# Up and down groups of an MLP woven job by job, with one more block pair of each up group in seven products

## The chip, the cores and the metric

The kernel runs on one NeuronCore of a Trainium2 chip. The metric is the device time of one execution in microseconds (us); for the kernel before it is the median of three runs. Engines are named as in the profile: PE (TensorE, matmuls), PEld (its weight loads), DVE (VectorE), ACT (ScalarE), POOL (GpSimd), SP (SyncE, which issues the DMAs).

## The reference

One layer of a trunk on x of 256 tokens by 2048 channels, float32. Two groups of heads (differential attention and an RWKV-7 recurrence) share one input projection, and one output projection adds to x; a squared-ReLU MLP follows.

```python
h = rms_norm(x, norm_mix[l])
proj = jnp.einsum('btd,de->bte', h, w_in[l])
...
mixed = jnp.concatenate([a_out, y], axis=-1)
x = x + jnp.einsum('bte,ed->btd', mixed, w_out[l])
h2 = rms_norm(x, norm_mlp[l])
u = jnp.square(jax.nn.relu(jnp.einsum('btd,df->btf', h2, mlp_up[l])))
x = x + jnp.einsum('btf,fd->btd', u, mlp_down[l])
```

D_MODEL is 2048 and D_FF 8192; mlp_up is 2048 x 8192 and mlp_down 8192 x 2048.

## The kernel before

**Split products.** Every weight is loaded as a float32 tile raw of 256 rows by 512 columns (a job; on chip 128 partitions x 1024). ACT casts it to hi, DVE subtracts to lo, and activations are kept as a high and a low unit in the same way. A product of a 128-row block is three matmuls: high by hi, high by lo, low by hi. A plain job is two row blocks by two halves of the tokens by three matmuls: 12 matmuls of 512 columns (`gemm`, L571). There are four tiles raw (NRAW) and three each of hi and lo (LOOK + 1).

**Seven products.** For the up projection's column groups from the fourth on (QUICK = 3), the jobs whose number within the group stands in FAST are done by a scheme of seven block products in place of eight (`seven`, L545): 21 matmuls of 256 columns. For them `split` (L517) builds, on DVE, four sums T of the weight's quarters, casts them to Th on ACT and subtracts to Tl on DVE; `normal_h` (L1449) builds the sums S of the activations once for each FAST job. The group then has four PSUM banks, and `join` (L1483) adds them up into C.

**Groups.** An up group i (16 of them, 8 jobs) makes 512 columns of the hidden layer: PE's products, a ReLU into z, a transpose, a square and the split into a unit u. A down group (32 of them, 4 jobs) multiplies two units u with a block of mlp_down and adds 256 x 512 results to x2. In the kernel before, the program writes whole groups one after the other: up, down, down, up, down, down.

**Order.** The program only records instructions (Recorder, L65). `plan` (L195) then sets the order of every engine's queue with costs and latencies of its own: it takes the instruction that can start first by its clock, and among those that could start at once the lowest rank. What `split` records has its rank lowered by SPL, so it goes ahead. Matmuls of attention and recurrence (transposes of tiles, small products, all in banks sm and tr) are side products that the plan puts between the main ones. An instruction with an anchor cannot be planned before the PE instruction that was recorded last before it; anchors bind instructions under hold and some DMAs.

Names in rows: raw, hi, lo, T, Th, Tl as above; xT, hT, hN, y, a, u are activation units; acc and side are PSUM banks of main products, four each, and sm and tr share the side banks; v, Am, Rm, X, UV, ao, pr belong to the recurrence and the attention; sq and sums to the first norm.

Of the kernel before, what the change touches and what calls it, by code (L numbers as in the profile page):

```python
# [14 lines left out]
F32R = mybir.dt.float32r  # L15
# [17 lines left out]
NRAW = 4  # L33
LOOK = 2
EV = 13
FAST = (1, 2, 4, 5, 7)
QUICK = 3

SPL = 120
KEEP = 0.3  # L40
WIN = 1.5
BD = 2.0
BA = 2.0

# [74 lines left out]
class Op:  # L119
    def __init__(self, eng, fname, fn, args, kw, rank):  # L120
        self.eng, self.fname, self.fn, self.args, self.kw, self.rank = eng, fname, fn, args, kw, rank
        aps = [a for a in args if isinstance(a, bass.AP)]
        self.outs = [aps[0]] + [kw[k] for k in ("accum_out",) if kw.get(k) is not None]
        self.ins = aps[1:] + [v for k, v in kw.items() if isinstance(v, bass.AP) and k != "accum_out"]
        n = int(np.prod(list(aps[0].shape)[1:]))
        self.dma = 0
        if fname == "dma_start":
            self.dma = n * aps[0].shape[0] * 4
            self.cost = 0.45
            self.small = min(a.ap[-1][1] for a in aps[:2]) < 128  # L130
        elif eng == "tensor":
            if fname == "transpose":
                self.cost = 0.11
            elif aps[1].dtype in (F32R, BF16):
                self.cost = 0.0056 + max(n, 64) * 0.000443
            else:
                m = aps[1].shape[-1]
                self.cost = 0.008 + max(n, m) * 0.00166
                if m <= 64:
                    self.cost = 0.06  # L140
        elif eng == "vector":
            m = int(np.prod(list(aps[1].shape)[1:])) if len(aps) > 1 else n
            single = fname in ("tensor_scalar", "tensor_copy") and aps[1].space != PSUM
            self.cost = 0.068 + max(n, m) * (0.00052 if single else 0.0063 if fname == "reciprocal" else 0.00104)
            if fname == "tensor_scalar" and aps[1].space == PSUM:
                self.cost += 0.16
            if fname == "tensor_tensor_scan":
                self.cost += 0.25
            if fname == "scalar_tensor_tensor" and len(aps) > 3:
                self.cost += 0.05  # L150
        elif eng == "scalar":
            self.table = {AF.Sqrt: 1, AF.Tanh: 2, AF.Exp: 2}.get(kw.get('func', args[2] if len(args) > 2 else None), 0) if fname == 'activation' else 0
            self.cost = (0.065 if aps[1].space == PSUM else 0.095) + n * 0.000833 + 0.085 * (len(self.ins) - 1 + len(self.outs) - 1)
            if aps[0].shape[0] <= 64:
                self.cost += 0.11
        else:
            self.cost = 0.1 + n * 0.001
        self.deps, self.users, self.left, self.ready = set(), [], 0, 0.0
        self.tiles = []
        self.bulk = eng == "tensor" and fname == "matmul" and aps[1].dtype == F32R and n == 512  # L160
        if eng == "tensor":
            self.load = min(1.0, n * (0.000417 if aps[1].dtype in (F32R, BF16) else 0.00083 if fname == "transpose" else 0.00167) / self.cost)
            self.load *= aps[1].shape[0] / P


class Together:
    def __init__(self, parts, rank):
        self.eng, self.fname, self.parts, self.rank, self.dma, self.bulk = "tensor", "together", parts, rank, 0, False
# [26 lines left out]
def plan(ops):  # L195
# [3 lines left out]
    tiles = {}  # L199
    for i, op in enumerate(ops):  # L200
        op.i = i
        if op.anchor and (op.hold or op.dma and op.outs[0].tensor.name.split("_")[0] != "raw"):
            op.deps.add(op.anchor)
        for write, aps in ((False, op.ins), (True, op.outs)):
            for ap in aps:
# [53 lines left out]
    while len(out) < len(ops):  # L259
# [77 lines left out]
def record(ctx, tc, A, nc):  # L337
# [138 lines left out]
                advance(t)  # L476

    w_in, w_out, w_up, w_dn = A["w_in"], A["w_out"], A["up"], A["down"]
    turn = [0]
# [11 lines left out]
    def fast(job):  # L491
        return job[0] is w_up and job[2] >= 512 * QUICK and job[1] // 256 in FAST

    jobs += up_jobs(0) + up_jobs(1)
    for e in range(8):
        for j in range(4):
            if e < 7 and not j % 2:
                jobs += up_jobs(2 * e + 2 + j // 2)
            jobs += [(w_dn, e * 1024 + 256 * k, 512 * j, 512) for k in range(4)]
    raws, parts = deque(), deque()  # L500

    def load(between=None):
# [42 lines left out]
    def seven(acc, u, k, S, B, first, last):  # L545
# [6 lines left out]
            return [u[:, i, k + kk, t * P:(t + 1) * P] for i in range(2)]  # L552

        def s(i):
            return [S[:, j, i] for j in range(2)]

        def b(kk, n):
            return [x[:, kk, n * 256:n * 256 + 256] for x in (hi, lo)]
# [12 lines left out]
    def gemm(units, w, c0, ncols, evac, side=False, hooks={}, off=0):  # L571
        turn[0] += w is w_up or w is w_dn
        quick = [j for j in range(8) if fast((w, 256 * j, c0))]
        acc = [bank("side" if turn[0] % 2 else "acc") for _ in range(4 if quick else 2)]
        nu = 4 if w is not w_out and w is not w_dn else 2
        nh = 2 * nu
        for j in range(nh):
# [8 lines left out]
            if j in quick:  # L586
                seven(acc, units[j // 2], 2 * j % 4, sums_[FAST.index(j)], (hi, lo, *T_), j == quick[0], j == quick[-1])
                done(2)
                continue
            for kk in range(2):  # L590
                k = 2 * j + kk
                u = units[off + j // 2]
                for t in range(2):
# [4 lines left out]
                    nc.tensor.matmul(o, xh, hi[:, kk, :ncols], start=(k == 0), stop=False, **more)  # L598
                    nc.tensor.matmul(o, xh, lo[:, kk, :ncols], start=False, stop=False, **more)
                    nc.tensor.matmul(o, xl, hi[:, kk, :ncols], start=False, stop=(k == 2 * nh - 1), **more)  # L600
        evac(acc)

    def rsqrt_small(out, ss, scale, bias):

# [827 lines left out]
        squares(x2[j], parts2, j)  # L1432

    rows2 = []

    def rstd_rows():

# [11 lines left out]
    def normal_h(j):  # L1449
# [7 lines left out]
        for p in range(2):  # L1457
            if 2 * j + p in FAST:

                S, sr = ftile([P, 2, 4, P], "S", F32R), ftile([P, 4, P], "sr")  # L1460
# [5 lines left out]
                nc.scalar.copy(S[:, 0], sr)  # L1466
                nc.vector.tensor_sub(S[:, 1], sr, S[:, 0])
                sums_.append(S)
                done()
        done()  # L1470
# [6 lines left out]
    us = []  # L1477
    pend = []

    def up_group(i, hooks):  # L1480
# [48 lines left out]
        gemm(hN if i > 1 else hT, w_up, 512 * i, 512, f, hooks=hooks)  # L1529

    def store_evac(j):
        def f(acc):
# [12 lines left out]
    for e in range(8):  # L1545
        for j in range(4):
            if e < 7 and not j % 2:
# [92 lines left out]
```

## Time and profile before

| | us |
|---|---|
| median of three runs | 1192.0 (1191.72 to 1192.01) |
| the profiled execution | 1192.01 |
| its span on the core | 1190.2 |
| PE busy in the span | 1179.4 |
| PEld busy | 979.9 |
| DVE busy | 974.1 |
| ACT busy | 844.8 |

The granted TensorE clock is full in all forty slices of the page. A share of busy time is a mean over stages. PE's ends are modelled: a matmul of 512 columns shows some 0.39 us and the next one starts 0.23 us later, so rates are read from the starts. The start comes first (weights and x arrive), then the projections with attention and recurrence in between, up to some 490 us, then the MLP.

### The profile page before, as it was taken

What the parts mean: (1) busy time and instruction counts of PE and PEld (TensorE: products, weight loads), DVE (VectorE), ACT (ScalarE), POOL (GpSimd) and SP (SyncE); (2) the same over time, 40 slices, a digit from 0 to 9 for tenths busy, and PEclk for the clock granted to TensorE, in tenths of its full rate; (3) what the DMA queues carried; (4) which work ended last, traced back from release to release, by engine and by line L of the source; (5) the groups of instructions that cost most, each with busy time, mean ns of one, the idle gap of its engine ahead of it and who ended that gap; (6) DMA issues with size and microseconds to landing.
All of it is one profiled execution on the core that took longest, in us unless ns stands there. A gap on an engine that the chain in (4) does not pass through costs nothing.

```text
span 1190.2 us, 18141 instructions
## 1 busy us (share of the span) xinstructions
PE 1179.4 (99%) x6649; PEld 979.9 (82%) x6649; DVE 974.1 (82%) x1579; ACT 844.8 (71%) x1421; POOL 7.3 (1%) x31
## 2 busy tenths in 40 slices
PE   9999999999999999999999999999999999999998
PEld 6887887888778778788888888888888888888886
DVE  7789594896975976798988988988988998898864
ACT  7784566855687768999686777687677677677652
POOL 2000000000000000000000000000000000000000
PEclk9999999999999999999999999999999999999999
DMA  8655656256455445656666666666666666666663
GB/s 279 205 159 164 172 162 184 85 165 175 128 169 172 141 142 184 180 169 194 188 198 199 184 203 198 194 190 197 212 176 196 198 192 182 208 180 197 207 205 132
DMA packets 126297, 216.20 MB, mean 182 GB/s; under 512 B 21824, under 2 KB 24384, under 8 KB 126208
## 3 DMA queue, kind: packets, MB, share of 16 engines
q1 hardware_dynamic: 126208, 215.05, 60.0%
q8 instruction: 52, 0.85, 0.3%
q14 instruction: 37, 0.30, 0.1%
HBM read 211.09 MB, written 3.93 MB: 181 GB/s over the span
## 4 chain that ended last, share of the span: by engine, by line
PE 77%; DVE 10%; ACT 7%; DMA 3%; issue 3%; SPq 0%; DVEq 0%; ACTq 0%
PE acc L334 47%; PE side L334 23%; DVE lo L334 4%; PE sm L334 3%; PE tr L334 3%; ACT z L334 2%; ACT hi L334 2%; DVE Tl L334 2%; DVE T L334 2%; PE sm L179 2%; DMA raw<-up 1%; DMA raw<-w_in 1%; DVE x L334 1%; DVE uf L334 0%; DVE u L334 0%
## 5 line engine op out<-in xcount | busy, mean ns | idle before, releaser
L334 DVE TENSOR_TENSOR lo<-raw,hi 128x1024 fp32r<-128x1024 f32 (+3 forms) x460 | 462.7, 1015 | 151.3 <-ACT hi L334 148.7
L334 ACT CAST hi<-raw 128x1024 fp32r<-128x1024 f32 (+2 forms) x395 | 405.0, 1033 | 164.2 <-PE acc L334 106.8
L334 PE MATMUL acc<-hi,xT 128*128 128x512 f32 (+1 forms) x832 | 267.6, 396 | 0.6 <-ACT hi L334 0.6
L334 PEld LDWEIGHTS acc<-hi,xT 128*128 128x128 f32 x832 | 154.6, 190 | 33.8 <-ACT hi L334 1.7
L334 PE MATMUL acc<-lo,xT 128*128 128x512 f32 (+1 forms) x416 | 164.0, 394 | 0.7 <-DVE lo L334 0.6
L334 PE MATMUL acc<-hi,u 128*128 128x512 f32 x512 | 163.2, 395 | 0.0
L334 PE MATMUL side<-hi,u 128*128 128x512 f32 x512 | 163.1, 395 | 0.0
L334 ACT ACTIVATE z<-C 32x128 f32<-32x128 f32 x338 | 104.2, 308 | 39.4 <-DVE C L334 35.0
L334 ACT CAST Th<-T 128x1024 fp32r<-128x1024 f32 x65 | 68.2, 1050 | 71.0 <-DVE T L334 70.3
L334 PEld LDWEIGHTS acc<-hi,u 128*128 128x128 f32 x512 | 96.4, 188 | 22.4 <-DVE u L334 0.3
L334 PEld LDWEIGHTS side<-hi,u 128*128 128x128 f32 x512 | 96.5, 188 | 22.2
L334 PE MATMUL side<-lo,u 128*128 128x512 f32 x256 | 101.0, 395 | 0.0
L334 PE MATMUL acc<-lo,u 128*128 128x512 f32 x256 | 101.0, 394 | 0.0
L334 PEld LDWEIGHTS acc<-lo,xT 128*128 128x128 f32 x416 | 78.9, 190 | 18.2 <-DVE lo L334 2.2
L334 PE MATMUL side<-hi,hN 128*128 128x512 f32 (+1 forms) x328 | 91.7, 353 | 0.0
L334 PE MATMUL acc<-hi,hN 128*128 128x512 f32 (+1 forms) x308 | 83.4, 343 | 0.0
L334 DVE TENSOR_TENSOR Tl<-T,Th 128x1024 fp32r<-128x1024 f32 x65 | 79.1, 1216 | 0.0
L334 PEld LDWEIGHTS side<-hi,hN 128*128 128x128 f32 x328 | 59.7, 188 | 9.5
L334 PEld LDWEIGHTS acc<-hi,hN 128*128 128x128 f32 x308 | 55.5, 188 | 7.8
L334 PE MATMUL side<-lo,hN 128*128 128x512 f32 (+1 forms) x164 | 57.9, 353 | 0.0
L334 PEld LDWEIGHTS acc<-lo,u 128*128 128x128 f32 x256 | 48.2, 188 | 11.0
L334 PEld LDWEIGHTS side<-lo,u 128*128 128x128 f32 x256 | 48.2, 188 | 11.0
(310 smaller groups left out, 1874.0 us busy)
## 6 DMA issues: line engine op xcount, KB each, us to landing
raw<-up SPq DMA_DIRECT2D x128, 512.0 KB, 3.8
raw<-down SPq DMA_DIRECT2D x128, 512.0 KB, 4.4
raw<-w_in SPq DMA_DIRECT2D x93, 512.0 KB, 3.8
raw<-w_out SPq DMA_DIRECT2D x32, 512.0 KB, 3.9
raw<-w_in SPq DMA_DIRECT2D x8, 288.0 KB, 3.1
x<-x SPq DMA_DIRECT2D x4, 512.0 KB, 7.3
out<-x SPq DMA_DIRECT2D x8, 256.0 KB, 3.4
raw<-w_in SPq DMA_DIRECT2D x6, 256.0 KB, 5.8
```

Source lines behind the costliest of these rows:

```text
L179: p.fn(*p.args, **p.kw)
L334: op.fn(*op.args, **op.kw)
```

## The change

- FAST has six of eight jobs (1, 2, 3, 5, 6, 7) in place of five (1, 2, 4, 5, 7). Two of the six sums S live in small tiles that the recurrence has left (HOME).
- `gemm` becomes a generator `steps` that stops after each job. From the fourth up group on, one up group and two down groups (three beside the last two) are run job by job in an order written as a string of u and d; the loads follow the same order. The first three up groups run alone, the last four down groups too. Up groups use the banks acc (the second one side), down groups the banks side; before, groups took the two kinds in turn.
- `join` is ranked like `split`, and its last two additions of 256 columns become one of 512 whose PSUM operand is repeated.
- In `plan`, POOL's instructions (memsets that clear tiles) get anchors. A side product whose operand comes from another engine than PE is planned to be ready LATE = 1.0 us later than its operand.

```diff
-FAST = (1, 2, 4, 5, 7)
+FAST = (1, 2, 3, 5, 6, 7)
...
+LATE = 1.0
...
+        self.side = eng == "tensor" and not (fname == "matmul" and aps[2].tensor.name.split("_")[0] in ("hi", "lo", "Th", "Tl"))
...
-        if op.anchor and (op.hold or op.dma and op.outs[0].tensor.name.split("_")[0] != "raw"):
+        if op.anchor and (op.hold or op.eng == "gpsimd" or op.dma and op.outs[0].tensor.name.split("_")[0] != "raw"):
             op.deps.add(op.anchor)
...
-            u.ready = max(u.ready, done + lag(op, u.eng))
+            u.ready = max(u.ready, done + lag(op, u.eng) + (LATE if u.side and op.eng != "tensor" else 0.0))
...
+    def beside(i):
+        a = 2 * i - 6 + (i > 14)
+        return list(range(a, a + 2 + (i > 13))), ("ddududuududududu" if i < 14 else "dddududduddududuudud" if i < 15 else "dduduuduuduududddddd")
+    for i in range(3):
+        jobs += up_jobs(i)
+    for i in range(3, 16):
+        ds, order = beside(i)
+        ups, downs = up_jobs(i), [j for d in ds for j in down_jobs(d)]
+        jobs += [(ups if c == "u" else downs).pop(0) for c in order]
+    for d in range(28, 32):
+        jobs += down_jobs(d)
...
-        acc = [bank("side" if turn[0] % 2 else "acc") for _ in range(4 if quick else 2)]
+        acc = [bank(tag) for _ in range(4 if quick else 2)]
...
+            if j < nh - 1:
+                yield
         evac(acc)
+        yield
...
+                if len(sums_) in HOME:
+                    S = [sm.tile([P, 512], F32R, tag=g, bufs=1, name=nm("S")).rearrange("p (s t) -> p s t", s=4) for g in HOME[len(sums_)]]
...
+            nc.rank = -SPL
             nc.scalar.copy(q[:, 0], b2[:, lt])
...
-            nc.vector.tensor_add(C[:, 1, lt], C[:, 1, lt], b3[:, rt])
-            nc.vector.tensor_add(C[:, 1, rt], C[:, 1, rt], b3[:, rt])
+            c1 = C[:, 1].rearrange("p (n c) -> p n c", n=2)
+            nc.vector.tensor_add(c1, c1, b3[:, rt].unsqueeze(1).broadcast_to([P, 2, 256]))
+            nc.rank = 0
...
-    up_group(0, {2: lambda: make_h(3), 4: rstd_rows})
-    up_group(1, {2 * j: lambda j=j: normal_h(j) for j in range(4)})
...
-    for e in range(8):
-        for j in range(4):
-            if e < 7 and not j % 2:
-                up_group(2 * e + 2 + j // 2, {1: fin_hook})
-            gemm(us, w_dn, 512 * j, 512, store_evac(j) if e == 7 else add_evac(x2[j]), hooks={1: fin_hook}, off=2 * e)
+    for _ in up_group(2, {1: fin_hook}):
+        pass
+    for i in range(3, 16):
+        ds, order = beside(i)
+        gens = {"u": up_group(i, {}), "d": run(*(down_group(d) for d in ds))}
+        for c in order:
+            next(gens[c])
+    for _ in run(*(down_group(d) for d in range(28, 32))):
+        pass
```

How the order moves, at three places. First PE in the middle of an MLP group, at the end of a job in seven products (its last block product is Th and Tl by hN). Before, the next job in seven products of the same up group follows:

```order
L334 MATMUL side_1685<-Th_1700,hN_1070 128x256
L334 MATMUL side_1685<-Tl_1701,hN_1070 128x256
L334 MATMUL side_1685<-Th_1700,hN_1070 128x256
L334 MATMUL side_1686<-hi_1703,hN_1070 128x256
L334 MATMUL side_1686<-lo_1704,hN_1070 128x256
```

Now, after two such jobs, a job of a down group stands there:

```order
L337 MATMUL acc_1687<-Th_1708,hN_1062 128x256
L337 MATMUL acc_1687<-Tl_1709,hN_1062 128x256
L337 MATMUL acc_1687<-Th_1708,hN_1062 128x256
L337 MATMUL side_1717<-hi_1711,u_1447 128x512
L337 MATMUL side_1717<-lo_1712,u_1447 128x512
```

Up and down jobs of one group now alternate, and the down jobs have the banks side to themselves.

Second, PE in the recurrence: a step (X by Rm) and the next step of its chain (UV by tmbk), which needs what ACT and DVE make of the first. Before, with five main products (acc) between them:

```order
L179 MATMUL sm_396<-X_389,Rm_367 64x64 x8
L334 MATMUL acc_459<-lo_484,xT_130 128x512
L334 MATMUL acc_459<-hi_483,xT_130 128x512
L334 MATMUL acc_460<-hi_483,xT_130 128x512
L334 MATMUL acc_460<-lo_484,xT_130 128x512
L334 MATMUL acc_460<-hi_483,xT_130 128x512
L334 MATMUL tr_441<-XA,DA_381 128x256
L334 MATMUL tr_441<-XAL,DA_381 128x256
L334 MATMUL tr_441<-XA,DA_381 128x256
L179 MATMUL sm_407<-UV_278,tmbk_369 64x64 x8
```

Now:

```order
L182 MATMUL sm_396<-X_389,Rm_367 64x64 x8
L337 MATMUL acc_460<-hi_490,xT_130 128x512
L337 MATMUL acc_460<-lo_491,xT_130 128x512
L337 MATMUL acc_460<-hi_490,xT_130 128x512
L337 MATMUL acc_459<-hi_490,xT_130 128x512
L337 MATMUL acc_459<-lo_491,xT_130 128x512
L337 MATMUL acc_459<-hi_490,xT_130 128x512
L337 MATMUL acc_460<-hi_490,xT_130 128x512
L337 MATMUL acc_460<-lo_491,xT_130 128x512
L337 MATMUL acc_460<-hi_490,xT_130 128x512
L337 MATMUL tr_509<-con,pr_401 128x128
L182 MATMUL sm_407<-UV_278,tmbk_369 64x64 x8
```

Nine main products stand between the two steps now.

Third, ACT at the start of the program (hi are the casts of the fourth and fifth weight tiles, xT the activation units, sq squares for the first norm). Before:

```order
L334 CAST hi_117<-raw_85 128x1024
L334 ACTIVATE xT_123<-x_86,con 128x256 x4
L334 ACTIVATE lame_102<-lams_101 128x2
L334 CAST hi_120<-raw_87 128x1024
L334 ACTIVATE xT_130<-x_88,con 128x256 x4
```

Now:

```order
L337 ACTIVATE sq_20_98<-x_83 128x1024
L337 CAST hi_117<-raw_85 128x1024
L337 ACTIVATE xT_123<-x_86,con 128x256 x4
L337 ACTIVATE sq_20_98<-x_86 128x1024
L337 CAST hi_120<-raw_87 128x1024
L337 ACTIVATE lame_102<-lams_101 128x2
L337 ACTIVATE xT_130<-x_88,con 128x256 x4
```

Two squares have moved ahead of these two casts; they stood behind the casts of later tiles.

## Rows read from the trace of the kernel before

**Rows 1.** The page: busy time of each engine, share of the span.

```profile
PE 1179.4 (99%) x6649; PEld 979.9 (82%) x6649; DVE 974.1 (82%) x1579; ACT 844.8 (71%) x1421; POOL 7.3 (1%) x31
```

**Rows 2.** Timeline of PE: start, time of one or several, operation, operands, count.

```profile
712.64 0.28 PE L334 MATMUL side<-hi,hN 128*128 128x256 f32 x1
...
715.13 0.40 PE L334 MATMUL side<-hi,hN 128*128 128x512 f32 x1
...
1110.57 0.28 PE L334 MATMUL acc<-hi,hN 128*128 128x256 f32 x1
...
1113.85 0.39 PE L334 MATMUL acc<-hi,hN 128*128 128x512 f32 x1
...
1180.01 0.39 PE L334 MATMUL acc<-lo,u 128*128 128x512 f32 x1
...
1185.58 0.40 PE L334 MATMUL acc<-lo,u 128*128 128x512 f32 x1
```

**Rows 3.** PE's waits over the whole span: releaser, us in total, times, longest.

```profile
PE tr L334 <- DVE v L334: 1.3, 1, 1.3
...
PE acc L334 <- DVE Tl L334: 0.7, 2, 0.5
...
PE sm L334 <- DVE Am L334: 0.3, 1, 0.3
```

**Rows 4.** Windows by stage: us; PE, PEld, DVE, ACT, POOL busy (count); clock; DMA; GB/s.

```profile
0.00:490.00 490.00, 485.12 (x3005) 389.37 (x3006) 375.05 (x656) 343.13 (x609) 7.32 (x31) 1.00 0.57 168
490.00:620.90 130.90, 129.93 (x611) 106.40 (x610) 114.15 (x185) 109.66 (x200) 0.00 (x0) 1.00 0.62 185
620.90:1141.40 520.50, 519.56 (x2845) 448.11 (x2844) 460.69 (x717) 377.35 (x600) 0.00 (x0) 1.00 0.64 195
```

**Rows 5.** Windows of half groups: up, down, and the up half at 1110 us.

```profile
620.90:641.80 20.90, 20.90 (x143) 19.28 (x142) 20.34 (x33) 13.64 (x15) 0.00 (x0) 1.00 0.68 204
641.80:664.10 22.30, 22.30 (x99) 18.09 (x98) 18.18 (x30) 17.81 (x37) 0.00 (x0) 1.00 0.62 187
...
1097.40:1119.10 21.70, 21.17 (x143) 19.34 (x142) 21.14 (x33) 14.44 (x16) 0.00 (x0) 1.00 0.66 196
```

**Rows 6.** DVE's groups by form, 600 to 1100 us: busy us, mean ns | idle before.

```profile
L334 DVE TENSOR_TENSOR lo<-raw,hi 128x1024 fp32r<-128x1024 f32 x127 | 153.8, 1218 | 46.1 <-ACT hi L334 45.2
L334 DVE TENSOR_TENSOR Tl<-T,Th 128x1024 fp32r<-128x1024 f32 x56 | 68.1, 1216 | 0.0
L334 DVE TENSOR_TENSOR T<-raw,T 128x256 f32<-128x256 f32 x113 | 47.2, 418 | 0.4
L334 DVE TENSOR_TENSOR T<-raw 128x512 f32<-128x512 f32 x57 | 39.1, 686 | 9.3 <-DMA raw<-up 9.2
L334 DVE TENSOR_TENSOR lo<-raw,hi 128x512 fp32r<-128x512 f32 x56 | 38.3, 683 | 0.0
...
L334 DVE TENSOR_TENSOR lo<-raw,hi 128x256 fp32r<-128x256 f32 x56 | 23.4, 417 | 0.0
...
L334 DVE TENSOR_TENSOR C<-C,acc 128x256 f32<-128x256 f32 x12 | 4.5, 413 | 0.0
```

**Rows 7.** Timelines of ACT, DVE and PE at the start (idle time before, releaser).

```profile
13.95 1.05 ACT L334 CAST hi<-raw 128x1024 fp32r<-128x1024 f32 x1
...
18.70 1.22 DVE L334 TENSOR_TENSOR lo<-raw,hi 128x1024 fp32r<-128x1024 f32 x1
...
19.98 0.50 PE L334 MATMUL acc<-lo,xT 128*128 128x512 f32 x1 [0.55 <-DVE lo L334]
```

**Rows 8.** DVE's waits, 600 to 1100 us.

```profile
DVE lo L334 <- ACT hi L334: 45.2, 53, 1.8
DVE T L334 <- DMA raw<-up: 9.2, 13, 0.9
```

**Rows 9.** Timeline of PE at the last transposes of ao.

```profile
438.55 1.06 PE L334 MATMUL tr<-con,ao 128*128 128x128 f32 x8
...
445.51 0.40 PE L334 MATMUL acc<-hi,a 128*128 128x512 f32 x1
```

More of the change, by code (lines that the diff above doesn't have):

```diff
@@ L167, in __init__ @@
     def __init__(self, parts, rank):
-        self.eng, self.fname, self.parts, self.rank, self.dma, self.bulk = "tensor", "together", parts, rank, 0, False
+        self.eng, self.fname, self.parts, self.rank, self.dma, self.bulk, self.side = "tensor", "together", parts, rank, 0, False, True
         self.args, self.kw = (), {}
@@ L478, in record @@
     w_in, w_out, w_up, w_dn = A["w_in"], A["w_out"], A["up"], A["down"]
-    turn = [0]
     jobs = []
@@ L492, in fast, with down_jobs @@
         return job[0] is w_up and job[2] >= 512 * QUICK and job[1] // 256 in FAST
-    jobs += up_jobs(0) + up_jobs(1)
-    for e in range(8):
-        for j in range(4):
-            if e < 7 and not j % 2:
-                jobs += up_jobs(2 * e + 2 + j // 2)
-            jobs += [(w_dn, e * 1024 + 256 * k, 512 * j, 512) for k in range(4)]
+    def down_jobs(d):
+        return [(w_dn, d // 4 * 1024 + 256 * k, d % 4 * 512, 512) for k in range(4)]
+    def beside(i):
[9 more added lines that the diff above has]
+        jobs += down_jobs(d)
     raws, parts = deque(), deque()
@@ L554, in s @@
         def s(i):
-            return [S[:, j, i] for j in range(2)]
+            return [S[j][:, i] for j in range(2)]
         def b(kk, n):
@@ L569, in seven, with gemm, steps @@
             nc.tensor.matmul(o, x[1], y[0], start=False, stop=end, skip_group_check=True)
-    def gemm(units, w, c0, ncols, evac, side=False, hooks={}, off=0):
-        turn[0] += w is w_up or w is w_dn
+    def gemm(*args, **kw):
+        for _ in steps(*args, **kw):
+            pass
+    def steps(units, w, c0, ncols, evac, side=False, hooks={}, off=0, tag="acc"):
         quick = [j for j in range(8) if fast((w, 256 * j, c0))]
-        acc = [bank("side" if turn[0] % 2 else "acc") for _ in range(4 if quick else 2)]
+        acc = [bank(tag) for _ in range(4 if quick else 2)]
         nu = 4 if w is not w_out and w is not w_dn else 2
@@ L588, in gemm @@
                 done(2)
-                continue
-            for kk in range(2):
+            for kk in range(0 if j in quick else 2):
                 k = 2 * j + kk
@@ L1434, in record @@
     rows2 = []
+    HOME = {0: ("DW", "DA"), 1: ("X", "Sp")}
     def rstd_rows():
@@ L1458, in normal_h @@
             if 2 * j + p in FAST:
-                S, sr = ftile([P, 2, 4, P], "S", F32R), ftile([P, 4, P], "sr")
+                sr = ftile([P, 4, P], "sr")
+                if len(sums_) in HOME:
+                    S = [sm.tile([P, 512], F32R, tag=g, bufs=1, name=nm("S")).rearrange("p (s t) -> p s t", s=4) for g in HOME[len(sums_)]]
+                else:
+                    S = ftile([P, 2, 4, P], "S", F32R)
+                    S = [S[:, 0], S[:, 1]]
                 a1, a2 = a[:, 2 * p], a[:, 2 * p + 1]
@@ L1465, in normal_h @@
                 nc.vector.tensor_sub(sr[:, 3], a2[:, :P], sr[:, 1])
-                nc.scalar.copy(S[:, 0], sr)
-                nc.vector.tensor_sub(S[:, 1], sr, S[:, 0])
+                nc.scalar.copy(S[0], sr)
+                nc.vector.tensor_sub(S[1], sr, S[0])
                 sums_.append(S)
@@ L1478, in record, with up_group @@
     pend = []
-    def up_group(i, hooks):
+    def up_group(i, hooks, tag="acc"):
         def join(acc):
@@ L1528, in f @@
             pend.append(fin)
-        gemm(hN if i > 1 else hT, w_up, 512 * i, 512, f, hooks=hooks)
+        return steps(hN if i > 1 else hT, w_up, 512 * i, 512, f, hooks=hooks, tag=tag)
     def store_evac(j):
@@ L1540, in fin_hook, with down_group, run @@
             pend.pop(0)()
-    up_group(0, {2: lambda: make_h(3), 4: rstd_rows})
-    up_group(1, {2 * j: lambda j=j: normal_h(j) for j in range(4)})
-    done()
-    for e in range(8):
-        for j in range(4):
-            if e < 7 and not j % 2:
-                up_group(2 * e + 2 + j // 2, {1: fin_hook})
-            gemm(us, w_dn, 512 * j, 512, store_evac(j) if e == 7 else add_evac(x2[j]), hooks={1: fin_hook}, off=2 * e)
+    def down_group(d):
+        e, j = d // 4, d % 4
+        return steps(us, w_dn, 512 * j, 512, store_evac(j) if e == 7 else add_evac(x2[j]), hooks={1: fin_hook}, off=2 * e, tag="side")
+    def run(*gens):
+        for g in gens:
+            yield from g
+    for _ in run(up_group(0, {2: lambda: make_h(3), 4: rstd_rows}),
+                 up_group(1, {2 * j: lambda j=j: normal_h(j) for j in range(4)}, "side")):
+        pass
+    done()
+    for _ in up_group(2, {1: fin_hook}):
+        pass
+    for i in range(3, 16):
[4 more added lines that the diff above has]
+    for _ in run(*(down_group(d) for d in range(28, 32))):
+        pass
 def _constants(par):
```

## The prediction

> **What bounds the kernel now.** I read the page's busy shares first: TensorE (PE) is busy 99% of the span, VectorE (DVE) 82%, ScalarE (ACT) 71%, GpSimd (POOL) 1% [rows 1]. By that, time goes only where PE has fewer products or waits less. The Trainium skill (Perfetto Trace Analysis, "Identifying the Most-Contended Engine") warns that the matmul busy share is a poor measure because matmuls are pipelined. The rows bear it out here, so I went on to start times.
>
> In the timeline a pair of weight rows done in seven products (21 matmuls of 256 columns, the S, Th and Tl forms among them) takes 715.13 - 712.64 = 2.49 us. Plain products of 512 columns follow each other every 5.57 / 24 = 0.232 us (1180.01 to 1185.58, eight threes), so a plain pair of 12 is 2.79 us. But the pair that began at 1110.57 took 3.28 us to 1113.85: a stall of 0.8 us [rows 2]. The list of PE's waits shows only two such waits for Tl, 0.7 us in all [rows 3]. The stage table tells the whole: 620.90 to 1141.40 holds twelve groups (one up group with five pairs in seven products, two down groups), 520.5 us, 43.38 each [rows 4]. Without a wait a group is 5 x 2.49 + 11 x 2.79 = 43.14 us. So 12 x 43.14 = 517.7, and 2.8 us are lost to waits.
>
> Who is late there? In the half group that holds the up products DVE is busy 20.34 of 20.90 us, and 97% still where the long stall was (21.14 of 21.70). In the half with the down products it is busy 18.18 of 22.30 [rows 5]. DVE makes the low parts (lo, Tl) of all weights; it is the bound in one half and idle in the other.
>
> Before the MLP, PE is idle 4.9 us of 490 [rows 4]. The largest wait is one of 1.3 us of a small transpose for DVE's v, and there are several of 0.3 [rows 3]: side products that stood in PE's order a little before their operands were there.
>
> **The change, part by part.** The time is counted against the profiled execution, 1192.01 us with a span of 1190.2; the median is 1192.0, so nothing has to be shifted.
>
> *One pair more in seven products.* Thirteen groups (columns from the fourth on), one pair each: 13 x (2.79 - 2.49) = -3.9 us on PE. The order bears it out: 78 casts to Th against 65. The Trainium skill (Perfetto Trace Analysis, "Matmuls") says that larger matmuls are more efficient than smaller ones, which speaks against this trade. The rows show 2.49 where seven eighths of 2.79 would be 2.44, so the narrow form costs 0.05 us a pair; without that the gain would be 4.5.
>
> Each such pair costs DVE 0.69 + 2 x 0.42 + 0.68 + 0.42 + 1.22 = 3.84 us in place of one lo of 1.22, so +2.6 a group. The join gives back 2 x 0.41 - 0.68 = 0.15, with the 512-wide addition priced by the lo of that size; its repeated operand is not shown, bounds 0.41 to 0.82 [rows 6]. ACT gets one more cast of Th in a group in which it has room. The sixth sum S costs DVE at most 4 x 0.42 + 0.68 = 2.4 us, once, before the first such group, hidden behind plain products.
>
> *Weaving.* Same jobs, same transfers; SP issues the weights in the new order. DVE's work per group is now 460.69 / 12 = 38.4 us [rows 4]; with the above, at most 40.9, and a group without waits is 6 x 2.49 + 10 x 2.79 = 42.84: 95%, evenly spread, where now one half stands at 97%. The order shows a down job after most fast pairs, and at most two fast pairs in a row, as before. So I let the 2.8 us go and, since 95% is little room, put new waits of 1.0 in their place (bounds 0, and 2.8, as many as now). Between 490 and 620.9 PE is idle 1.0 us [rows 4], in part for DVE in the first group of this kind; I take 0.5 back, bounds 0 and 1.0.
>
> The up groups now always use the four acc banks, so the join must have read them before the next up job begins two down jobs (5.6 us) later. It is some 3 us of DVE work and goes ahead by rank. If a weight transfer holds DVE first, PE waits for the rest.
>
> *Side operands planned 1 us later (LATE).* No instruction is added. Where five main products stood between one step of the chain and the next, nine stand now, 2.1 us in place of 1.2. The waits of 1.3 and 0.3 go, and two or three of that kind: -2.2 us; bounds 0 (they move to the next operand) and -2.9 (4.9 idle less some 2.0 of the start).
>
> *Clearings after their work.* POOL's memsets move by a few places and now wait for slots; POOL has 7.3 us of work in the span [rows 1], so I cost them at nothing. What hides them is POOL's idleness. If that failed, a side chain would start late, not the main products.
>
> *The start.* The plan now puts a Square of 1024 ahead of the cast of the fourth weight tile and another ahead of the fifth's, and a sum on DVE ahead of the fourth lo. That cast began at 13.95, the fifth lo at 18.70, and PE waited 0.55 for it at 19.98 [rows 7], so this place has no room. The Square moves the fourth hi and lo by about 1 us, of which PE had 0.2 in hand, and the fifth by less. Then the transfers set the pace. I take +0.7 us, bounds 0 and +1.9 (two Squares).
>
> **Sum:** -3.9 - 2.8 + 1.0 - 0.5 - 2.2 + 0.7 = -7.7, **1184.3 us**. With the good bounds 1192.0 - 3.9 - 2.8 - 1.0 - 2.9 = 1181.4; this case's own range is 1180.5 to 1187.5.
>
> **Rivals.**
> *Only the columns count.* The waits move from one place to another: DVE's Tl is late at the two fast pairs that still follow each other, and the planner's new slack for side products is used up by other operands. 1192.0 - 3.9 + 0.7 = 1188.8. For it: DVE at 95% has less room over a whole group than now (89%). Against it: the half with 97% is gone.
>
> *DVE becomes the bound (slower).* DVE works in order, and in 500 us it stood 45.2 us for ACT's hi and 9.2 us for a weight transfer [rows 8], 4.7 us a group. It has 42.84 - 40.9 = 1.9 us to spare. A hi is late mostly because the buffers are full and DVE ahead, which ends by itself; a T that stands at the head of the queue before its transfer has landed does not. If more than 2.5 us of the 4.7 stay, a group is longer than today's 43.38. With 3.0 it is 43.9: +0.5 x 13 = 6.5, with LATE and the start 1192.0 + 6.5 - 2.2 + 0.7 = 1197.0; with all 4.7 it would be about 1219.
>
> *LATE opens a gap at the end of the chain.* In the order of before 26 main products stand between the last transposes of ao and the first product with them; in the trace that is 438.55 to 445.51, 7 us [rows 9]. In the new order 12 stand there, 2.8 us, for two operations each of ACT and DVE, DVE's behind two lo and two additions (2 x 1.22 + 2 x 0.68 = 3.8 us) [rows 6]. If PE waits 2.2 us for these, and if the side waits stay as they are as well, the time is 1184.3 + 2.2 + 2.2 = 1188.7; with a second such gap 1190.9.
>
> *The change doesn't do what it says.* The order excludes it for the products; for the clearings it would change nothing.
>
> **How the numbers follow.** Forecast 0.62, columns only 0.22, DVE bound 0.08, gap 0.07, none of these 0.01. A measurement of this kernel can tell about 0.2%, 2.4 us, from no change: faster means under 1189.6. Faster: 0.62 + 0.17 (columns only, unless the start costs its 1.9) + 0.02 = 0.81; same: 0.05 + 0.05 + 0.01 of DVE = 0.11; slower: 0.07 + 0.01 = 0.08. The range is 1180.5 to 1190.0: down to the good bounds and a little for a start without its 0.55 wait, up to columns alone with the start at +1.9 (1192.0 - 3.9 + 1.9 = 1190.0). That leaves out the DVE bound and part of the gap.
>
> **What would show it.** The woven stage: groups of 42.9 to 43.0 us, DVE near 95% in both halves, single fast pairs at 2.49 and no row of Tl above 0.3 us in PE's waits. Groups at 43.4 would be the columns-only case, longer ones with DVE waiting for raw the bound. Before the MLP: no wait for v or Am of 0.3 or more, PE idle near 3 us of its 490. At the start: a wait for lo some 0.7 us longer up to 25 us. At the last ao: no wait for a. I am wrong in kind if the woven stage is not shorter than before, and in the second term if it is shorter by the columns alone.

## The result: 1.1% slower, and the profile after

The changed kernel takes 1205.4 us (median of four, 1204.1 to 1207.1) where the kernel before takes 1191.9: ratio 1.011 [1.010, 1.013]. 1184.3 was forecast, with a range to 1190.0. The profiled execution took 1204.7 us with a span of 1202.9, 12.7 more than before.

From the page before: the chain of work that ended last, by engine, and the DMA issues of the MLP's weights (KB each, median us from issue to landing):

```profile
PE 77%; DVE 10%; ACT 7%; DMA 3%; issue 3%; SPq 0%; DVEq 0%; ACTq 0%
...
raw<-up SPq DMA_DIRECT2D x128, 512.0 KB, 3.8
raw<-down SPq DMA_DIRECT2D x128, 512.0 KB, 4.4
```

The page after, with the busy time first:

```profile
PE 1180.5 (98%) x6766; PEld 983.9 (82%) x6766; DVE 1008.7 (84%) x1636; ACT 857.0 (71%) x1435; POOL 7.8 (1%) x31
...
PE 49%; DVE 21%; DMA 9%; ACT 6%; issue 4%; DVEq 0%; SPq 0%; ACTq 0%
...
raw<-up SPq DMA_DIRECT2D x128, 512.0 KB, 4.1
raw<-down SPq DMA_DIRECT2D x128, 512.0 KB, 4.1
```

Against [rows 1] DVE has 34.6 us more work and PE's share has fallen. The chain runs through DMA for 9% (3% before) and DVE for 21% (10%): transfers and what DVE makes of them now set the end in more places.

Windows after (columns as in [rows 4]): the stretch before the MLP, the opening of the MLP, and ten woven groups, from the last product with Th of one group's up jobs to that of the tenth group after it (the rows at 600.02 and 1045.29 below):

```profile
0.00:490.00 490.00, 485.27 (x3002) 389.40 (x3003) 376.21 (x655) 340.68 (x608) 7.85 (x31) 1.00 0.57 168
...
490.00:620.90 130.90, 128.81 (x644) 107.31 (x643) 119.76 (x201) 111.61 (x202) 0.00 (x0) 1.00 0.63 185
...
600.02:1045.29 445.27, 433.92 (x2463) 376.39 (x2461) 409.62 (x641) 324.83 (x511) 0.00 (x0) 1.00 0.62 189
```

PE's timeline before, the first product with hN, and the two starts that bound the same ten groups:

```profile
531.76 0.41 PE L334 MATMUL side<-hi,hN 128*128 128x512 f32 x1
...
598.47 0.27 PE L334 MATMUL acc<-Th,hN 128*128 128x256 f32 x1
...
1031.84 0.28 PE L334 MATMUL acc<-Th,hN 128*128 128x256 f32 x1
```

PE's timeline after, the same product and the two starts:

```profile
532.52 0.39 PE L337 MATMUL acc<-hi,hN 128*128 128x512 f32 x1
...
600.02 0.28 PE L337 MATMUL acc<-Th,hN 128*128 128x256 f32 x1
...
1045.29 0.28 PE L337 MATMUL acc<-Th,hN 128*128 128x256 f32 x1
```

A woven group takes 44.53 us; without waits it would be 42.84. Measured in the same way the groups before took 43.34 (598.47 to 1031.84). So the place is plain: the first product with hN comes 0.76 us later, and ten groups are 10 x 1.19 = 11.9 us longer, together 12.7. Between the two PE takes 0.8 us more than before, and behind the tenth group 0.8 less, which cancel. DVE works 409.62 of these 445.27 us, 41.0 a group.

PE's waits from 540 to 1100 us, then DVE's from 620 to 1100 (us in total, times, longest), after:

```profile
PE side L337 <- DVE lo L337: 7.2, 10, 0.8
PE side L337 <- ACT hi L337: 4.2, 5, 1.3
PE side L337 <- DVE u L337: 0.8, 1, 0.8
PE acc L337 <- DVE z L337: 0.6, 1, 0.6
PE side L337 <- ACT u L337: 0.2, 1, 0.2
```

```profile
DVE T L337 <- DMA raw<-up: 17.3, 22, 2.3
DVE Tl L337 <- ACT Th L337: 13.3, 21, 1.1
DVE lo L337 <- ACT hi L337: 5.3, 7, 1.9
```

Before, DVE stood 45.2 us for hi and 9.2 for a transfer in 500 us [rows 8]; from 620 to 1100 us it was 41.8 and 8.5. The wait for hi is nearly gone, the wait for transfers has doubled, and a wait of Tl for ACT's Th, 13.3 us, is new. The timelines show how the wait for a transfer reaches PE. DVE at the start of a group, then before its ninth job, which is a plain down job behind two fast up jobs (jobs in seven products) in a row; then ACT and PE there:

```profile
645.50 0.41 DVE L337 TENSOR_TENSOR q<-q,acc 128x256 f32<-128x256 f32 x1
646.59 0.69 DVE L337 TENSOR_TENSOR T<-raw 128x512 f32<-128x512 f32 x1 [0.68 <-DMA raw<-up]
647.20 0.41 DVE L337 TENSOR_TENSOR q<-q,acc 128x256 f32<-128x256 f32 x1
...
662.49 1.28 DVE L337 TENSOR_TENSOR x<-x,side 128x512 f32<-128x512 f32 x2
663.78 0.69 DVE L337 TENSOR_SCALAR z<-C 32x128 f32<-32x128 f32 x3
664.58 1.25 DVE L337 STREAM_TRANSPOSE uf<-z 128x1024 f32<-128x1024 f32 x1
665.75 2.32 DVE L337 TENSOR_TENSOR lo<-raw,hi 128x1024 fp32r<-128x1024 f32 x2
```

```profile
661.34 3.19 ACT L337 ACTIVATE z<-C 32x128 f32<-32x128 f32 x10
664.55 2.00 ACT L337 CAST hi<-raw 128x1024 fp32r<-128x1024 f32 x2
```

```profile
665.65 0.50 PE L337 MATMUL side<-hi,u 128*128 128x512 f32 x1
666.99 0.51 PE L337 MATMUL side<-lo,u 128*128 128x512 f32 x1 [0.83 <-DVE lo L337]
```

T waits 0.68 us for its transfer in the middle of the join, whose second addition stands behind it. Until 665.75 DVE then has almost no pause, so the delay travels on, and the lo of the ninth job comes 0.83 us late. ACT is in it too: its ReLUs z need the C that this join makes, ten of them stand ahead of the cast hi of the ninth job, and lo can start only behind that cast. In five of the ten groups PE waits for this hi itself (4.2 us of the list above, longest 1.3) and then for lo.

### The profile page after: what moved, and what is told of

Read it like the earlier page. It is cut to its first block, busy times and chain, and to the rows that moved or that the text cites. A ratio compares the mean times of both kernels' runs of the same rounds, so it can differ in the third digit from the quotient of the medians.

```text
span 1202.9 us, 18459 instructions
## 1 busy us (share of the span) xinstructions
PE 1180.5 (98%) x6766; PEld 983.9 (82%) x6766; DVE 1008.7 (84%) x1636; ACT 857.0 (71%) x1435; POOL 7.8 (1%) x31
## 4 chain that ended last, share of the span: by engine, by line
PE 49%; DVE 21%; DMA 9%; ACT 6%; issue 4%; DVEq 0%; SPq 0%; ACTq 0%
PE acc L337 29%; PE side L337 13%; DVE lo L337 10%; DMA raw<-up 9%; DVE T L337 4%; DVE Tl L337 3%; ACT z L337 3%; PE sm L337 3%; PE tr L337 2%; PE sm L182 2%; ACT Th L337 2%; DVE C L337 2%; ACT hi L337 1%; DVE z L337 1%; DVE u L337 1%
## 5 line engine op out<-in xcount | busy, mean ns | idle before, releaser
L337 PE MATMUL side<-hi,u 128*128 128x512 f32 x1024 | 338.4, 397 | 5.1 <-ACT hi L337 4.2
L337 PEld LDWEIGHTS side<-hi,u 128*128 128x128 f32 x1024 | 193.3, 189 | 49.4 <-ACT hi L337 5.4
L337 PE MATMUL side<-lo,u 128*128 128x512 f32 x512 | 204.1, 399 | 7.2 <-DVE lo L337 7.2
L337 PE MATMUL acc<-hi,hN 128*128 128x512 f32 (+1 forms) x584 | 158.3, 335 | 0.6 <-DVE z L337 0.6
L337 PE MATMUL acc<-lo,hN 128*128 128x512 f32 (+1 forms) x292 | 97.7, 335 | 0.0
L337 PE MATMUL acc<-Th,S 128*128 128x256 f32 x468 | 96.0, 281 | 0.0
L337 PEld LDWEIGHTS acc<-Th,S 128*128 128x128 f32 x468 | 77.2, 188 | 0.0
L337 DVE TENSOR_TENSOR T<-raw,T 128x256 f32<-128x256 f32 x156 | 65.6, 422 | 1.6
L337 PE MATMUL acc<-Tl,S 128*128 128x256 f32 x234 | 65.9, 282 | 0.3 <-DVE Tl L337 0.3
L337 PEld LDWEIGHTS acc<-lo,hN 128*128 128x128 f32 x292 | 55.0, 188 | 8.8
```

The costliest lines, as they stand in the source:

```text
L337: op.fn(*op.args, **op.kw)
```

## The experiments

Queue theory: the plan lets transfers land too soon, T stands at the head of DVE's queue for a transfer that is not there, and holds what lies behind. Its rivals: DVE has no room for six pairs whatever the order (full), and the weaving itself, or the two fast pairs in a row, makes operands late (weave, place). A group is measured over ten groups as above; "T" is DVE's wait of T for raw, 620 to 1100 us; "landing" says by how many us later than in the changed kernel the plan lets transfers land, all of them or those of the MLP alone.

| run | pairs, order | landing | group us | T us | time us | ratio to before |
|---|---|---|---|---|---|---|
| after | six, woven | as planned | 44.53 | 17.3 | 1205.4 | 1.011 [1.010, 1.013] |
| e1 | five, woven | as planned | 44.12 | 36.1 | 1199.9 | 1.008 [1.006, 1.009] |
| e2 | six, grouped | as planned | 43.78 | 8.9 | 1201.7 | 1.009 [1.007, 1.010] |
| e3 | six, woven | all +0.7 | 43.73 | 8.6 | 1202.5 | 1.009 [1.008, 1.011] |
| e4 | six, woven, no LATE | as planned | 44.56 | 16.8 | 1206.6 | 1.013 [1.011, 1.014] |
| e5 | five, woven | MLP +0.7 | 43.12 | 2.2 | 1193.6 | 1.002 [1.001, 1.003] |
| e6 | six, woven | MLP +0.7 | 43.53 | 7.0 | 1195.4 | 1.004 [1.002, 1.005] |
| e7 | six, woven, no Tl | as planned | 44.35 | 57.1 | 1204.0 | 1.011 [1.009, 1.012] |
| e8 | before (five, grouped) | MLP +0.7 | 43.71 | - | 1195.6 | 1.004 [1.002, 1.005] |
| e9 | six, woven, no Tl | MLP +0.7 | 43.04 | 5.3 | 1190.3 | 0.998 [0.998, 0.999] |
| e15 | six, spread | as planned | 43.72 | 10.6 | 1197.3 | 1.006 [1.004, 1.007] |
| e18 | six, woven | MLP +1.2 | 43.65 | 0.3 | 1196.0 | 1.004 [1.002, 1.005] |

### Five pairs, grouped order, landing, LATE (e1 to e4)

e1 takes the pairs of before in the new order, e2 the new pairs in the order of before:

```diff
# e1
-FAST = (1, 2, 3, 5, 6, 7)
+FAST = (1, 2, 4, 5, 7)
# e2
-... ("ddududuududududu" if i < 14 else ...
+... ("dddddddduuuuuuuu" if i < 14 else ...
# e3
-            done = dma + 0.9
+            done = dma + 1.6
# e4
-LATE = 1.0
+LATE = 0.0
-        if op.anchor and (op.hold or op.eng == "gpsimd" or op.dma and ...
+        if op.anchor and (op.hold or op.dma and ...
```

(e2: the last two strings likewise.) In the plan a transfer of 512 KB lands 1.1 + 1.46 + 0.9 = 3.5 us after its issue; the page has 4.1. That is why e3 adds 0.7.

> The woven kernel with five pairs of each up group in seven products (1, 2, 4, 5, 7, as before) in place of six. Theory A (a weight transfer at the head of DVE's queue: the sum T that stands inside the join waits for its tile, and what DVE loses there comes out at PE's next plain job): the waits of T stay at some 1.5 us a group, PE still loses about 1 us a group, groups of 44.0 us or more, 1203 us or more. Theory B (DVE is full: with six pairs it has nothing left to make up a late T): the same waits of T are absorbed, groups of 43.1 to 43.3, 1190 to 1193 us. Theory C (the weave itself puts too much into one half): as A, 1203 or more.

> Six pairs in seven products, but whole groups one after the other as in the kernel before (down, down, up); everything else as changed. Theory B: the up half would need 20.3 + 2.3 = 22.6 us of DVE for 20.5 us of products, so PE waits 2 us or more a group, groups of 44.5 or more, 1205 us or more. Theory C: without the weave groups of 43.0 to 43.4, 1188 to 1192 us. Theory A alone: about 0.8 us of T waits a group as before, groups of 43.0 to 43.5.

> The changed kernel with one number of the plan altered: a transfer is planned to land 0.7 us later (the plan has 1.1 + 1.5 + 0.9 = 3.5 us from issue to landing of a 512 KB tile, the profile 4.1). Theory A: DVE's waits of T for a transfer fall from 17.3 us (620 to 1100) to 5 or less, PE's recurring wait for hi and lo goes, groups of 42.9 to 43.4, 1187 to 1193 us. Theory B or C: groups stay at 44.2 or more, 1202 us or more.

> The changed kernel without LATE and without the anchors of the clearings. If these two cost time in the first part (the MLP's first products with hN began at 532.5 us, 531.8 before), the first hN is at 531.8 or earlier and the whole is about 1 us shorter, 1203 to 1204; if LATE gained and the start lost, the waits for v and Am are back, the start is as before, and the whole is within 1 us of 1205. In either case the woven groups stay at 44.2 or more.

Every theory got a part. With five pairs the woven order still loses 1.0 us a group, and T waits 36.1 us (the profiled execution of e1 took 1203.1 us, 3.3 more than its median, so the 1.0 is on the high side); with six pairs the grouped order loses 0.9, to Tl. e3 takes 0.8 a group off, but the part before the MLP, whose transfers it also moved, lost 3.1 us (first product with hN at 535.66). e4 shows that LATE is not what lengthens the groups, which stay at 44.56. The first product with hN comes at 531.72, 0.8 earlier, but PE then waits 2.0 us for u in place of 0.2, and the whole is not shorter.

### Which cause: landing of the MLP alone, and DVE relieved (e5 to e9)

```diff
# e5 (five pairs), e6 (six), e8 (the kernel before), e9 (no Tl)
-            done = dma + 0.9
+            done = dma + (1.6 if op.ins[0].tensor.name in ("up", "down") else 0.9)
# e7, e9
...
-                nc.vector.tensor_sub(Tl, Tr, Th)
-                parts[-1] += (Th, Tl)
+                parts[-1] += (Th, Th)
```

> Five pairs of eight in seven products, woven (as in the run with five woven pairs: 1199.9 us, groups of 44.16 us in the mean against 43.14 without waits), with one line more: in the plan's own clock the MLP's weight transfers (up and down) land 0.7 us later, the other transfers as they were. Queue theory (a T that stands at the head of DVE's queue before its transfer has landed holds all behind it): the waits of DVE's T for raw, 36.1 us there, fall under 10, the groups come to 43.2 to 43.4, and the time to about 1199.9 - 13 x 0.85 = 1189. Weave theory (the order of the jobs itself makes operands late, whatever DVE's room): groups stay at 43.9 or more, time 1197 or more. Full theory (DVE has no room): five pairs leave it 4.8 us a group, so it expects the same as the queue theory here, and the difference at six pairs.

> The changed kernel with the same line: only the MLP's weight transfers are planned to land 0.7 us later. Where all transfers were planned so, groups fell to 43.76 us but the part before the MLP lost 3.1 us. Queue theory: groups of 42.9 to 43.1, time 1184 to 1186. Full theory (with 40.9 us of work in 42.84 DVE catches up with nothing): groups stay near 43.7, DVE waits for raw under 9 us, and the time is that of the run with all transfers less 3.1, about 1199. Neither expects the first product with hN later than 533.

> The changed kernel without the subtraction that makes Tl, the low part of T: the products that took Tl take Th in its place (this part of the computation is left out), so PE has the same number of products and DVE 6 x 1.22 = 7.3 us less a group, 33.6 of 42.84. Full theory: DVE gets room to catch up after each late transfer; groups of 42.9 to 43.2 although T still waits for raw (17.3 us or more over the stretch), time 1184 to 1188. Queue theory alone: the late T holds the lo behind it as long as before whatever DVE's room; groups stay at 44 or more, time over 1200.

> The kernel before with the same line: the MLP's weight transfers planned to land 0.7 us later. Its PE order stays as it is, DVE's changes. Queue theory: T's waits for raw fall from 9.2 us to under 4 and the groups from 43.38 towards 43.14: 1189 to 1191.5. If the kernel before lost its 0.24 us a group to Tl and DVE's full half instead, the time is 1191 to 1193, no difference that can be told. Over 1195 would say that a later planned transfer costs by itself, and part of what is seen in the woven kernels with it.

> The changed kernel without the subtraction that makes Tl (that part of the computation is left out, Th stands in its place), and with the MLP's weight transfers planned to land 0.7 us later. With each of the two alone the groups were 43.5 us (landing) and 44.4 (no Tl); without waits they are 42.84. If DVE's missing room is what is left once the transfers are planned late enough, the groups come to 42.9 here, T waits for raw under 10 us, time 1186 to 1188. If DVE's room is no part of it, they stay at 43.4 to 43.6 and the time at 1194 to 1196.

e5 settles the weave: 43.12 us a group where 43.14 was worked out, no loss at all. The order of the jobs was not the trouble by itself, and the groups with five pairs need nothing but the later landing. The time missed its forecast of 1189 all the same (1193.6): PE waits 2.3 us for u and 0.7 for z in the opening, and the first product with hN comes 1.2 later than in the kernel before. e6 met neither forecast: its groups lie between those of the queue theory (42.9 to 43.1) and those of the full theory (near 43.7).

e7 is the sharpest. By the durations DVE has 7.3 us a group less to do, by its busy time 6.2 (34.7 where it was 41.0), and 0.2 us a group is gained. Ten groups of e7, and DVE's waits there, 620 to 1100 us:

```profile
601.16:1044.69 443.53, 430.36 (x2462) 373.70 (x2461) 347.28 (x581) 324.52 (x511) 0.00 (x0) 1.00 0.59 190
```

```profile
DVE T L337 <- DMA raw<-up: 57.1, 43, 3.1
DVE lo L337 <- ACT hi L337: 36.3, 34, 2.4
```

The planner puts T where it thinks that the transfer has landed; with DVE free earlier T stands there earlier, and the freed time is spent waiting, still ahead of everything else. Room is no cure for a queue that is blocked at its head. Together with the later landing room does help: 43.04 in e9 where e6 has 43.53 (e7 and e9 leave Tl out and are no kernels to keep). So at six pairs there is a second cause beside the landing. And a later landing is no gain by itself: in e8 the kernel before loses 0.37 us a group with it, by the starts to Tl, though T no longer waits at all. This was the forecast's third case, over 1195.

T's total wait does not measure the loss: e13 below waits 12.8 us and loses 0.4 us a group, e15 waits 10.6 and loses 0.9. The later landing moves more in the plan than T alone. That it takes away a part of the loss is shown; how much of this goes by the T in the join, which the timeline above shows, was not tried apart.

### DVE's costs and the opening (e10 to e12)

e10 is e6 with DVE's z 0.1 us and its additions to x 0.09 us longer in the plan; e11 also changes the opening; e12 is e11 without LATE and the clearings' anchors.

```diff
# e10 to e12
+            if fname == "tensor_scalar" and aps[0].shape[0] == 32 and aps[1].space != PSUM:
+                self.cost += 0.1
+            if aps[0].tensor.name[:2] == "x_" and aps[-1].space == PSUM:
+                self.cost += 0.09
# e11, e12: the opening
+        if i == 3:
+            return [0, 1], "uddduduududududu"
-    for _ in up_group(2, {1: fin_hook}):
+    for _ in up_group(2, {1: fin_hook}, "side"):
```

> Six woven pairs, the MLP's transfers planned to land 0.7 us later, and two of DVE's costs in the plan set to what the traces show: 0.1 us more for a z of 32 partitions (six a group) and 0.09 more for an addition to x (four a group), 0.96 us a group that the plan did not know. Nothing that is computed changes. Cost theory (what is left, 0.68 us a group, is this work that the plan laid in room that is not there): groups of 42.9 to 43.1, time 1187 to 1189. Full theory (no order helps, DVE cannot do it): 43.4 or more, 1194 or more.

> The kernel with the planned costs, and the opening of the woven stretch changed: the third up group uses the other four banks, so that the first woven group need not wait for its z, and in the first woven group one up job goes ahead of the first down job, which gives u 2.8 us more. It should take away the waits of PE for u (0.2 to 2.3 us in the woven runs at 555) and z (0.5 to 0.9 at 570): 1 to 1.5 us less than the kernel with the planned costs alone, 1185.5 to 1188. If those waits only move to the next operand, no difference.

> The kernel with planned costs and the changed opening, but without LATE and with the clearings no longer held to their place. If LATE costs what it seemed to (the first product with hN 0.8 us later), it is 0.8 us faster than with it, 1185 to 1187; the wait of 1.3 us for v is back. If it only moved waits, the two are within 0.5 us.

e10: 1195.9 us (1.004 [1.002, 1.005]), groups of 43.90, no gain; the cost theory falls. (Its profiled execution took 1198.3 us, and one of the ten groups 46.49; the other nine are 43.61 in the mean, close to e6's 43.53.) e11: 1195.3 (1.003 [1.002, 1.004]); the waits for u and z at 555 to 572 are gone, and a wait for Tl (0.4 at 573.9) and a longer one for lo (1.0 at 622.8, where e10 has 0.4) stand in their place: the forecast's second case, no difference from e10 beyond 0.6. e12: 1193.8 (1.002 [1.001, 1.003]); its first product with hN comes at 531.38 against 533.25. LATE with the anchors costs there, it does not gain. The time expected, 1185 to 1187, was not reached, since the groups stay at 43.70.

### The place: no two fast pairs in a row (e13 to e18)

```diff
# e13, e15, e16, e17
-FAST = (1, 2, 3, 5, 6, 7)
+FAST = (1, 2, 4, 5, 6, 7)
# e16 to e18: 2.1 in place of 1.6
+            done = dma + (2.1 if op.ins[0].tensor.name in ("up", "down") else 0.9)
```

In the string of a group the up jobs stand at places 3, 5, 7, 8, 10, 12, 14, 16: the jobs numbered 2 and 3 follow each other, and the change makes both fast. With 3 plain there are no two in a row. e13 is that with the landing +0.7, e12's opening and no LATE; e14 the same with five pairs; e15 has the new FAST alone; e16 is e13 with the landing +1.2, e17 that with e10's costs; e18 has the landing +1.2 alone.

> Six woven pairs as in the changed kernel, but the plain up jobs are the first and the fourth of eight (FAST 1, 2, 4, 5, 6, 7) where they were the first and the fifth: no two fast pairs follow each other any more. With the MLP's transfers planned to land 0.7 us later, the changed opening, and without LATE (the kernel of that kind with the old FAST: groups of 43.3 to 44.6, 1193.75 us). Place theory (the rest of the loss is the two fast pairs in a row, behind which the ninth job's lo comes late): groups of 42.85 to 43.0, 1185 to 1188. Total theory (DVE's work for six pairs does not fit): the wait moves to another job, groups at 43.3 or more, 1191 to 1194.

> Five woven pairs with the MLP's transfers planned to land 0.7 us later (groups of 43.13 us, 1193.6 us) and, new, the changed opening and no LATE. PE waited there 2.3 us for u at 555 and 0.7 for z at 575, and the first product with hN came 1.2 us later than in the kernel before. If these three are what keeps it above the kernel before, 1189 to 1190; if the wait for u moves to the next operand, 1191 to 1192.

> The changed kernel with one change: FAST 1, 2, 4, 5, 6, 7, so that no two fast pairs follow each other. Transfers planned as in it, LATE and the opening as in it. Queue theory with the first cause still there (transfers planned to land too soon): T waits for raw 15 us or more over the stretch and holds the queue; groups of 43.5 to 44.2, 1195 to 1201. If the place of the two fast pairs was the main cause by itself, groups of 43.0 and 1186 to 1188.

> The six spread pairs with the changed opening and without LATE, with the MLP's transfers planned to land 1.2 us later than in the changed kernel in place of 0.7. If single late transfers are what is left (T waits for raw 12.8 us over the stretch, longest 2.0), these waits halve, groups come to 42.9 and the time to 1186 to 1187.5. If planning T later only makes Tl late, PE's waits for Tl grow and the time is 1189 to 1192.

> The same with DVE's z of 32 partitions planned 0.1 us longer and its additions to x 0.09 us longer, as the traces show them. If the unplanned DVE work (0.96 us a group) is what lets single late transfers through to PE, it is 0.5 to 2 us faster than without; with two fast pairs in a row the same line changed nothing, and if that holds here too, the two are within 0.5 us.

> The changed kernel with one line: the MLP's transfers planned to land 1.2 us later (with 0.7: groups of 43.5 us, 1195.4). FAST, opening and LATE as in the changed kernel. If landing is the whole cause, groups come to 42.9 to 43.1 and the time to 1187 to 1189.5. If the two fast pairs in a row hold a part of their own, the wait for lo at the ninth job stays (0.3 us or more in each group), groups at 43.3 or more, 1193 to 1196.

| run | group us | T us | time us | ratio to before |
|---|---|---|---|---|
| e13 six spread, +0.7 | 43.21 | 12.8 | 1189.3 | 0.998 [0.997, 0.999] |
| e14 five, +0.7 | 43.13 | 1.9 | 1189.1 | 0.998 [0.997, 0.999] |
| e16 six spread, +1.2 | 42.80 | 0.4 | **1185.4** | 0.995 [0.994, 0.996] |
| e17 the same, costs | 42.99 | 0.3 | 1187.8 | 0.997 [0.996, 0.998] |

e13 met neither of its forecasts: its groups of 43.21 lie between the place theory (to 43.0) and the total theory (from 43.3). e14 came as expected if the opening was what kept e5 above the kernel before.

Four kernels make the table that settles it, in us a group: neither 44.53, landing alone (e18) 43.65, spread alone (e15) 43.72, both (e16) 42.80, the value without waits. Each takes 0.8 to 0.9, and they add. e16 also has the new opening and no LATE, which e15 and e18 have not. These hardly touch the groups: 44.56 in e4 against 44.53, and 43.13 in e14 against 43.12 in e5. In e18 T no longer waits, and PE no longer waits for hi there, yet the ninth job still waits for lo in every group. PE in e18, then the ten groups of e18 and of e16:

```profile
664.81 0.39 PE L337 MATMUL side<-hi,u 128*128 128x512 f32 x1
665.72 0.50 PE L337 MATMUL side<-lo,u 128*128 128x512 f32 x1 [0.52 <-DVE lo L337]
```

```profile
599.56:1036.05 436.49, 430.48 (x2462) 374.65 (x2461) 413.75 (x641) 324.75 (x511) 0.00 (x0) 1.00 0.62 193
```

```profile
598.56:1026.55 427.99, 427.99 (x2463) 374.81 (x2461) 413.95 (x641) 326.39 (x511) 0.00 (x0) 1.00 0.62 197
```

The two have the same DVE work (413.75 and 413.95) and the same products. In e16 DVE is busy 413.95 of 427.99 us, 97%, and PE never waits: the total fits, against the full theory. What did not fit was its place. Two fast pairs give PE only 2 x 2.49 us, while DVE needs 2 x 3.84 by the durations that the prediction took, and the additions to x, z and the transpose come on top. That this crowding is why the place matters is read from these sums and from DVE's timeline; what was tried is only which job is plain. e17 was a miss: DVE's costs closer to the trace, and 2.4 us slower, 1.9 of them in the ten groups. Why was not found; the plan's choices change in many places at once.

## Why the prediction was wrong, step by step

**One pair more, -3.9: right.** e14 with five pairs has groups of 43.13, e16 with six 42.80: 0.33 each where 0.30 was counted. In the changed kernel larger waits cover it.

**Weaving, -2.8 and +1.0: this step failed.** It let the old waits go and put 1.0 us of new ones for the whole stage. Its words were "95%, evenly spread", "So I let the 2.8 us go" and "at most two fast pairs in a row, as before". The 95% was about right (DVE's work is 41.0 to 41.4 a group where 40.9 was the bound), and a mean of 97% costs nothing in e16. But it was not evenly spread: two fast pairs in a row were named and then not priced (0.8 us a group), and T's waits for transfers were read [rows 8] and left to a rival. In place of 1.0 us of waits in the whole stage there were 1.69 a group, 16.9 in ten groups; a later landing takes 0.9 a group off (e18), the spread places 0.8 (e15), both together all of it (e16). ACT's room was taken from its total, too: at the ninth job it had none, and PE waited 4.2 us for its hi.

**The rival "DVE becomes the bound (slower)"** had the mechanism and the place: a T that stands at the head of the queue. With the 3.6 us a group that DVE was idle ((445.27 - 409.62) / 10) in place of its 3.0, its sum gives 1205.1. That this is so near is partly luck, for LATE's -2.2 stands in it. It was given 0.08, since most of DVE's waits, those for hi, were taken to end by themselves. They did; but the waits of T doubled, and the 13.3 us of Tl behind ACT's Th stood in no term. (With five pairs they cost nothing by themselves: e5 has 12.6 us of them and its groups lose nothing.) What was not done was to hold the plan's own landing, 3.5 us, against the page, which had 3.8 for up and 4.4 for down in the kernel before. And the name was wrong: DVE's total is not the bound, its queue is.

**The opening, -0.5: wrong.** Between 490 and 620.9 us PE is idle 2.1 us where it was 1.0: it waits there for u (0.8 and 0.2) and z (0.6), 1.6 us in all; nothing was given back. In e16 these waits are gone, with 0.7 for Tl and two of 0.3 for lo in their place.

**LATE, -2.2: wrong in sign, tried together with the clearings' anchors** (e4, and e12 against e11, where the first product with hN comes 0.8 and 1.9 us earlier without them). Of the 4.9 us that PE was idle in 490 us before, 4.7 are left. By the windows of the first 60 us (before, then after) the start took its part:

```profile
0.00:60.00 60.00, 57.44 (x278) 46.16 (x279) 42.49 (x79) 43.58 (x70) 6.48 (x29) 1.00 0.77 240
```

```profile
0.00:60.00 60.00, 56.36 (x275) 44.32 (x276) 41.58 (x79) 42.46 (x69) 1.89 (x16) 1.00 0.76 240
```

1.1 us more idle, where **the start** was put at +0.7 (bounds 0 and 1.9): right in kind, though not for the squares alone: without LATE and the anchors (e4) PE is busy 56.91 of these 60 us, so half of the 1.1 is theirs. The waits behind the start did shrink by 1.2, and still the first product with hN comes 0.76 later. Up to that product PE is idle 5.3 us before and after, so the 0.76 went into time in which PE counts as busy. Where exactly stays open. The rival of a gap at the last ao did not come: no wait for a is among PE's.

**The clearings, nothing:** they were only ever moved together with LATE, so this was not tried apart.

The best kernel, e16, has the groups that the forecast gave to the change: 42.80, with DVE at 97%. Its time, 1185.4 us, is near 1184.3 in part by luck, for it has no LATE and another opening. The forecast priced the weave as if the order had been that of e16.

## What to carry to other kernels

An engine that works in order is not read by its busy share: ask of each operation at the head of its queue whether its operand will be there, and hold a planner's own landing times against the page's. Give an operation that waits for a transfer a margin before giving the engine less work; e7 shows that freed time can turn into waiting alone. Try the margin, too: in the kernel before it cost 0.37 us a group (e8). Where work per job is uneven, price the densest two or three jobs in a row, not the mean of a group.

## What the runs showed that was not expected

- DVE busy 97% of ten groups (413.95 of 427.99 us) with no wait of PE in e16, and 78% (347.28 of 443.53 us) in e7 with groups of 44.35.
- The median landing of the same 512 KB transfer lay between 3.6 us (up, in e8) and 4.4 us (up, in e9; down, in the kernel before).
- DVE's durations in the timeline overlap: the lo that begins at 649.72 in the trace after shows 1.22 us, and the next operation starts at 650.86, 1.14 later. Sums of durations overstate DVE's work: over the ten groups after they make 44.9 us a group, and DVE is busy 41.0.
